# Gate and up projections by seven block products in place of eight, with sums of weight blocks made in DRAM, and a down projection in two groups

## The chip, the cores and the metric

The kernel runs on one core of one Trainium2 chip. The metric is the device time of one execution in microseconds (us), here the median of several runs. Engines: TensorE (PE in the profile; its weight loads PEld), VectorE (DVE), ScalarE (ACT), GpSimd (POOL) and SyncE (SP, which here only issues DMA).

## The reference

One layer of a decoder over 512 prompt tokens and 8 sample tokens (T = 520), model width 1024. Two attention mixers run on the same normalised input; the last part is what the change touches:

```python
m = gate_a * (oa @ w_pa) + gate_b * (ob @ w_pb)
x = x + m @ w_o
gu = _rmsnorm(x, norm2_g) @ w_gu              # w_gu [1024, 2 * 2816]
return x + (silu(gu[..., :D_FF]) * gu[..., D_FF:]) @ w_down
```

A final RMSNorm follows. Outputs are also the state rows of the caches (46 MB that only move along, DRAM to DRAM). All data is float32.

## The kernel before, in words

Everything is kept with features on the partitions and the 520 tokens along the free axis, in two halves of 256 and 264 columns (`SPAN`). A float32 product is made of three products of a rounded type: each operand is split into a high part and a low part, and `project_steps` issues high × high (L245), high × low (L246) and low × high (L248), for each of the chunks of 128 of the contraction and each half of the tokens.

The weights come as a list of `jobs`, one per block of 1024 × 128 (512 KB). For each job SP loads the block into one of three raw buffers (`load_plain`, L119), ScalarE makes the high part (`split_plain`, L137, `whi`) and VectorE the low part (L138, `wlo`). `weights(name)` queues the next job's split and up to four loads ahead. With each split `issue_copy` adds a rate to a counter, and whenever that passes 1 one of the 64 state copies is issued from ScalarE's queue (L112); `COPY_RATE` is 0.2 per job at first and 0.65 from job 44.

The stages from the middle on: the branch products with `w_pa` (PSUM tiles `pspa`, sums L1057 to L1060), the output projection with `w_o` (`pso`, residual L1089), norm 2 in two halves, then SwiGLU and down. Norm 2 takes the sum of squares per token on TensorE, its root on GpSimd (L1118, `rt`), spreads it by TensorE (`psr`), and VectorE makes the product with the gain (L1128, `h2f`), ScalarE and VectorE split it (L1129, L1130).

SwiGLU goes over 22 chunks of 128 features. Each has a gate and an up block: 8 chunks of contraction × 3 products × 2 halves = 48 matmuls each, 96 together (`psg`, `psu`). `gated` then takes silu on ScalarE (L1155), the product of gate and up on VectorE (L1156), and the split of the result (L1157, L1158), once for each half. Down is 8 output chunks m, each over all 22 chunks of features: 22 × 6 = 132 matmuls and two additions to the residual `x2` (L1266); the pieces of the final norm follow from `finish`, `emit` and `emit_last`.

A scheduler of the framework sets the order of the instructions on each engine from the program's order and its own estimates, before the kernel runs; each engine then works its list strictly in order, and waits where an instruction's inputs or buffers aren't ready.

Of the kernel before, what the change touches and what calls it, by code (L numbers as in the profile page):

```python
# [16 lines left out]
P = 128  # L17
# [6 lines left out]
SPAN = ((0, 256), (256, T))  # L24
HD = 64
# [11 lines left out]
COPY_FROM = 44  # L37
COPY_RATE = (0.2, 0.65)
# [14 lines left out]
POOLW = ("qb0", "qb1")  # L53


def trunk_kernel(tc, x_prompt, x_sample, cache_a, cache_b1, cache_b2, cache_b3, norm1_g, w_in, sinks,
# [8 lines left out]
    # ------------------------------------------------------------------ pools  # L65
# [14 lines left out]
    # ------------------------------------------------------------------ constants  # L80
# [10 lines left out]
    # ------------------------------------------------------------------ weights  # L91
    copies = []
    for b in range(NS):
# [5 lines left out]
        for r in range(0, 2047, 512):  # L99
            e = min(r + 512, 2047)  # L100
            copies.append((o_sb3[0, b, r:e], cache_b3[0, b, r + 1:e + 1]))
    copies.reverse()
    due = [0.0]

    def issue_copy(after, n):
        """State rows that only move along: DRAM to DRAM, paced by the weights."""
        due[0] += n
        with tc.issue_after(after.ins):
            while due[0] >= 1.0 and copies:
                due[0] -= 1.0  # L110
                o, i = copies.pop()
                nc.scalar.dma_start(o.rearrange("r a h d -> r (a h d)"), i.rearrange("r a h d -> r (a h d)"))  # L112
# [31 lines left out]
    def split_ff(raws, kc, name):  # L144
        return split_plain(raws, kc, name, pools["ff"], 2)

    def split_rope(cols):
        """Per 64-wide head a column offset; head dims d go to partition 2*(d%32)+d//32."""
# [15 lines left out]
    jobs = []  # (name, chunks of the contraction, loads, split)  # L164
# [48 lines left out]
    def split_to(n):  # L213
        while n_split[0] < min(n, len(jobs)):
# [4 lines left out]
            issue_copy(a, COPY_RATE[0 if i < COPY_FROM else 1])  # L219
# [3 lines left out]
    def weights(name, ahead=1):  # L223
        """Split weights of a job; the next job's split and the loads after it are queued first."""
# [56 lines left out]
    # ------------------------------------------------------------------ norm 1  # L281
# [48 lines left out]
    def norm_roots():  # L330
        """Per token the root of its mean square, as the diagonal of a matrix."""
# [15 lines left out]
    def half_x(h):  # L347
        """x of 256 tokens transposed, its product with the gain in two parts; the root per token comes after the projections."""
# [61 lines left out]
    # ------------------------------------------------------------------ pools of the two mixers  # L410
# [10 lines left out]
    def rope(ps2, dst, name, blocked=False):  # L421
        """ps2: PSUM [128, 2, 260]; dst [128, 520] gets the rotated values, prompt part in stride-4 blocks if asked."""
# [5 lines left out]
        nc.gpsimd.tensor_tensor(z, z, cos, op=ALU.mult)  # L428
# [745 lines left out]
    for m in range(2, NF):  # L1174
# [3 lines left out]
        for h in range(2):  # L1178
            gated(m, h, pgs[h], pus[h])
# [173 lines left out]
```

## Time and profile before

| | us |
|---|---|
| three runs | 918.91, 913.42, 915.9 |
| median | 915.9 |
| profiled execution, span from the first to the last instruction | 910.4 |
| TensorE busy in it | 883.6 |
| VectorE, ScalarE, GpSimd busy | 453.2, 340.4, 138.8 |
| DMA moved | 137.09 MB |

The profiled execution's span leaves out what lies before its first and after its last instruction, and is 5.5 us below the median of the runs. In the rows that the prediction shows, a group's row reads: line, engine, operation, output<-input, shapes, count | busy us in total, mean ns of one | idle us of the engine just before them and what ended it. A DMA row: what, queue, count, KB of each, median us from issue to landing. A window's row: from:to, length, busy us and count of each engine, the clock granted to TensorE, the share of the core's 16 DMA engines in use, GB/s. Matmuls overlap, so a matmul's own duration is longer than the time from one to the next.

### The profile page before, as it was taken

What the parts mean: (1) busy time and instruction counts of PE and PEld (TensorE: products, weight loads), DVE (VectorE), ACT (ScalarE), POOL (GpSimd) and SP (SyncE); (2) the same over time, 40 slices, a digit from 0 to 9 for tenths busy, and PEclk for the clock granted to TensorE, in tenths of its full rate; (3) what the DMA queues carried; (4) which work ended last, traced back from release to release, by engine and by line L of the source; (5) the groups of instructions that cost most, each with busy time, mean ns of one, the idle gap of its engine ahead of it and who ended that gap; (6) DMA issues with size and microseconds to landing.
All of it is one profiled execution on the core that took longest, in us unless ns stands there. A gap on an engine that the chain in (4) does not pass through costs nothing.

```text
span 910.4 us, 17130 instructions
## 1 busy us (share of the span) xinstructions
PE 883.6 (97%) x7104; PEld 833.4 (92%) x7104; DVE 453.2 (50%) x920; ACT 340.4 (37%) x750; POOL 138.8 (15%) x114
## 2 busy tenths in 40 slices
PE   6998989999999999999999999999999999999996
PEld 6898889878998788779999999999999999999995
DVE  4878648754597554724464653333333333233322
ACT  6324324444466655533233443222222222222222
POOL 2335553423232112100000200000000000000000
PEclk9999999999999999999999999999999999999998
DMA  9546745331332211488568339357356555657302
GB/s 298 174 129 189 216 147 181 100 99 47 94 117 94 72 32 60 124 195 233 157 208 272 93 114 278 113 184 229 114 177 194 155 167 174 194 162 235 90 19 95
DMA packets 149854, 137.09 MB, mean 151 GB/s; under 512 B 5344, under 2 KB 144768, under 8 KB 148368
## 3 DMA queue, kind: packets, MB, share of 16 engines
q1 hardware_dynamic: 145472, 83.65, 33.0%
q10 hardware_dynamic: 2592, 46.08, 14.7%
q0 software_dynamic: 1712, 6.26, 2.1%
q8 instruction: 56, 0.92, 0.4%
q14 instruction: 22, 0.18, 0.1%
HBM read 129.14 MB, written 51.86 MB: 199 GB/s over the span
## 4 chain that ended last, share of the span: by engine, by line
PE 83%; DMA 6%; DVE 5%; issue 3%; POOL 2%; ACT 1%; SPq 0%; POOLq 0%; DVEq 0%; ACTq 0%
PE psu L246 5%; PE psu L248 5%; PE psg L248 5%; PE psu L245 5%; PE psg L246 5%; PE psg L245 5%; PE psd L245 4%; PE psd L248 4%; PE psd L246 4%; PE poa L931 3%; DMA raw_wo<-in_w_o 2%; DMA qc<-q_dram 2%; PE psgb L248 2%; PE psgb L245 2%; PE psgb L246 2%
## 5 line engine op out<-in xcount | busy, mean ns | idle before, releaser
L245 PE MATMUL psd<-g_hi,whi_wd 128*128 128x256 f32 (+1 forms) x352 | 93.4, 285 | 0.5 <-DVE x L1266 0.5
L246 PE MATMUL psd<-g_lo,whi_wd 128*128 128x256 f32 (+1 forms) x352 | 93.1, 282 | 0.0
L246 PE MATMUL psu<-h_lo,whi_wu 128*128 128x256 f32 (+1 forms) x352 | 93.0, 283 | 0.0
L246 PE MATMUL psg<-h_lo,whi_wg 128*128 128x256 f32 (+1 forms) x352 | 92.6, 282 | 0.0
L245 PE MATMUL psu<-h_hi,whi_wu 128*128 128x256 f32 (+1 forms) x352 | 92.1, 282 | 0.0
L245 PE MATMUL psg<-h_hi,whi_wg 128*128 128x256 f32 (+1 forms) x352 | 91.6, 282 | 0.0
L248 PE MATMUL psd<-g_hi,wlo_wd 128*128 128x256 f32 (+1 forms) x352 | 74.5, 283 | 0.0
L248 PE MATMUL psu<-h_hi,wlo_wu 128*128 128x256 f32 (+1 forms) x352 | 73.5, 283 | 0.0
L248 PE MATMUL psg<-h_hi,wlo_wg 128*128 128x256 f32 (+1 forms) x352 | 73.4, 282 | 0.0
L245 PEld LDWEIGHTS psd<-g_hi,whi_wd 128*128 128x128 f32 x352 | 66.3, 188 | 0.8 <-DVE x L1266 0.7
L245 PEld LDWEIGHTS psu<-h_hi,whi_wu 128*128 128x128 f32 x352 | 66.3, 188 | 0.0
L246 PEld LDWEIGHTS psd<-g_lo,whi_wd 128*128 128x128 f32 x352 | 66.2, 188 | 0.0
L245 PEld LDWEIGHTS psg<-h_hi,whi_wg 128*128 128x128 f32 x352 | 66.1, 188 | 0.0
L246 PEld LDWEIGHTS psu<-h_lo,whi_wu 128*128 128x128 f32 x352 | 66.1, 188 | 0.0
L246 PEld LDWEIGHTS psg<-h_lo,whi_wg 128*128 128x128 f32 x352 | 66.1, 188 | 0.0
L138 DVE TENSOR_TENSOR wlo_wg<-raw_wg,whi_wg 128x1024 fp32r<-128x1024 f32 x22 | 27.0, 1225 | 74.4 <-ACT whi_wg L137 69.8
L248 PEld LDWEIGHTS psd<-g_hi,wlo_wd 128*128 128x128 f32 x352 | 55.9, 188 | 0.0
L138 DVE TENSOR_TENSOR wlo_wd<-raw_wd,whi_wd 128x1024 fp32r<-128x1024 f32 (+1 forms) x24 | 27.3, 1137 | 57.1 <-ACT whi_wd L137 56.2
L248 PEld LDWEIGHTS psu<-h_hi,wlo_wu 128*128 128x128 f32 x352 | 55.6, 188 | 0.0
L248 PEld LDWEIGHTS psg<-h_hi,wlo_wg 128*128 128x128 f32 x352 | 55.6, 188 | 0.0
L137 ACT ACTIVATE whi_wd<-raw_wd 128x1024 fp32r<-128x1024 f32 (+1 forms) x24 | 23.7, 989 | 84.6 <-PE psd L246 67.9
L1156 DVE TENSOR_TENSOR sg<-sg,psu 128x256 f32<-128x256 f32 (+1 forms) x44 | 16.9, 421 | 72.5 <-PE psu L248 72.5
(371 smaller groups left out, 2465.6 us busy)
## 6 DMA issues: line engine op xcount, KB each, us to landing
raw_wg<-in_w_gu SPq DMA_DIRECT2D x22, 512.0 KB, 3.9
raw_wu<-in_w_gu SPq DMA_DIRECT2D x22, 512.0 KB, 5.3
raw_wd<-in_w_down SPq DMA_DIRECT2D x16, 512.0 KB, 5.5
out<-in_cache_b_kv ACTq DMA_DIRECT2D x8, 1022.0 KB, 5.5
out<-in_cache_b_kv ACTq DMA_DIRECT2D x8, 512.0 KB, 4.0
raw_qa<-in_w_in SPq DMA_DIRECT2D x8, 512.0 KB, 3.8
raw_ga<-in_w_in SPq DMA_DIRECT2D x8, 512.0 KB, 4.8
raw_gb<-in_w_in SPq DMA_DIRECT2D x8, 512.0 KB, 3.9
```

Of the source, the lines that this page charges most:

```text
L137: a = nc.scalar.activation(hi[:, :kc], raw[:, :kc], AF.Copy)
L138: nc.vector.tensor_tensor(lo[:, :kc], raw[:, :kc], hi[:, :kc].bitcast(F32), op=ALU.subtract)
L245: nc.tensor.matmul(ps[i], hi[:, k], xh[:, k0 + k, sl], start=st, stop=False)
L246: nc.tensor.matmul(ps[i], hi[:, k], xl[:, k0 + k, sl], start=False, stop=False)
L248: last_mm[0] = nc.tensor.matmul(ps[i], lo[:, k], xh[:, k0 + k, sl], start=False, stop=en).ins
L931: nc.tensor.matmul(po[64 * kv:64 * kv + 64, :], va[:, j - 1 + r, 64 * kv:64 * kv + 64], pts_[kv, r], start=(r == rel[0]), stop=(r == 1), s ...
L1156: nc.vector.tensor_tensor(sg, sg, pu, op=ALU.mult)
```

## The change

Tokens: from the output projection on the halves are 260 and 260 columns (`SPAN2`). Norm 2 writes its result in quarters: two halves of the features times two halves of the tokens (`hq`, `hb_hi`, `hb_lo`).

Gate and up: chunks 0 and 1 (`NCL = 2`) are computed as before. For each of the other 20 ("units" 2 to 21) the gate block and the up block, each cut in two along the contraction, and the two token halves form a 2 × 2 block product, which is computed with seven block products (q1 to q7) in place of eight. A product is 4 chunks × 3 matmuls of 260 columns: 12; a unit 84. Three of the seven use a block of `w_gu` as it stands, four use a sum of blocks: s1 = a21 + a22, s2 = a11 + s1, s3 = a11 + a21, s4 = a12 + s2 (with signs put into the token side). These sums are made in DRAM: four tensors of 512 × 2560, each in four row blocks of 1.31 MB, by 16 plain copies on ScalarE's queue and 16 adding transfers on GpSimd's queue (`add_rows`). They are entries ahead of the 64 state copies in the same paced list, 96 in all. An adding transfer waits until its copy, and any sum that it reads, is there. The pace is 0.3 per job, 1.0 from job 18, 0.8 from job 56, then 0.15 per piece of a unit and 1.2 per piece of down.

The token side needs sums too: `sums_of_tokens` makes four sums of 1040 columns on VectorE, and splits four results on ScalarE and VectorE. The products' results are combined on VectorE (L1371 to L1382), with three activations on ScalarE (L1369, L1377, L1381) and one split of 520 columns (L1245, L1246).

A piece is a tile that holds the blocks of two products (two loads of 256 KB, L1313) or a block of down; four raw buffers and four pairs of `whi`/`wlo` hold them (L1325, L1326). Unit loads become 70 tiles of 512 KB where 40 blocks were.

Down: after unit 9 all 8 output chunks m are taken over the feature chunks 0 to 7 (48 matmuls each), and at the end all 8 over chunks 8 to 21 (84 each). So each m adds to `x2` twice.

The core of the diff:

```diff
+HH = T // 2
+SPAN2 = ((0, HH), (HH, T))
...
-COPY_RATE = (0.2, 0.65)
...
+NCL = 2
+SUM_RATE = (0.3, 1.0, 0.8)
+SUM_FROM, SUM_TO = 18, 56
+STEP_RATE = {"u": 0.15, "d": 1.2}
...
+    sums_d = {q: dram.tile([512, WS], F32, name=f"sum_{q}") for q in ("s1", "s2", "s3", "s4")}
...
+    sums = sum_step("s1", "a21", 0) + sum_step("s3", "a11", 0) + sum_step("s1", "a22", 1) + sum_step("s2", "a11", 0)
+    sums += sum_step("s3", "a21", 1) + sum_step("s4", "a12", 0) + sum_step("s2", "s1", 1) + sum_step("s4", "s2", 1)
+    copies = sums + copies
...
+    def add_rows(dst, src, r, add):
+        o, i = (quarter[n][P * r:P * r + P] for n in (dst, src))
+        if add:
+            with tc.issue_after(last_pool[0]):
+                last_pool[0] = nc.gpsimd.dma_start(o, i, accum_op=ALU.add, max_dma_last_dim=4 * WS // 2).ins
+        else:
+            nc.scalar.dma_start(o, i)
...
-            issue_copy(a, COPY_RATE[0 if i < COPY_FROM else 1])
+            issue_copy(a, SUM_RATE[(i >= SUM_FROM) + (i >= SUM_TO)])
...
+    AQ = {"q1": "a11", "q2": "a12", "q3": "s4", "q4": "a22", "q5": "s1", "q6": "s2", "q7": "s3"}
...
+        tt(hq[:, 0], hq[:, 0], hq[:, 3], op=ALU.subtract)
+        split(0)
+        yield
+        tt(hq[:, 3], hq[:, 3], hq[:, 2], op=ALU.subtract)
+        tt(hq[:, 2], hq[:, 2], hq[:, 0], op=ALU.add)
+        split(2)
+        yield
+        tt(hq[:, 1], hq[:, 1], hq[:, 2], op=ALU.subtract)
+        split(1)
+        split(3)
...
+            back = [("u", n - 1, "q3")] if n > a else []
+            steps_ += [("u", n, "q1")] + back + [("u", n, q) for q in ("q5", "q6", "q4", "q7", "q2")]
+        steps_.append(("u", b - 1, "q3"))
+        for m in range(NK):
+            steps_ += [("d", m, k0) for k0 in ((0,) if a == NCL else (FIRST, FIRST + 8))]
...
+            raw = pool.tile([P, NK, P], F32, tag="raw", name=f"rawp{i}", bufs=bufs)
+            k = 0
+            for _, src, kc in pieces[i]:
+                nc.sync.dma_start(raw[:, k:k + kc], src.rearrange("(k p) n -> p k n", p=P))
...
+        i = piece_of[s]
+        load_pieces(i + 4)
+        split_pieces(i + 3)
+        load_pieces(i + 5)
+        return w_of.pop(s)
...
+            if q == "q1":
+                nc.scalar.activation(self.s1, self.a, AF.Copy)
+            if q == "q6":
+                tt(self.v, self.b, self.s1, op=sub)
+            if q == "q7":
+                tt(self.c21, self.b, self.s1, op=sub)
+                tt(self.c22, self.c21, self.e, op=sub)
+                tt(self.c21, self.c21, self.f, op=add)
+            if q == "q2":
+                nc.scalar.activation(self.s1, self.a, AF.Silu)
+                tt(self.c21, self.c21, self.s1, op=ALU.mult)
+            if q == "q3":
+                tt(self.v, self.e, self.v, op=sub)
+                nc.scalar.activation(self.v, self.v, AF.Silu)
+                tt(self.c22, self.c22, self.v, op=ALU.mult)
+                split_g(self.n, self.z)
...
-            project(pds, weights(f"wd{m}_{k0}"), kc, g_hi, g_lo, k0=k0, first=k0 == 0, last=k0 + kc == NF)
+            project_d(pds, operand(s), 0, n, (0, 1), True, True)
```

How the order of the instructions changes is shown at three places. First VectorE in the steady part of gate and up. In before, for chunks 7 to 10 (`sg` the gated product, its two digits' last the half; `wlo_wg`, `wlo_wu` the low parts of the gate and up blocks):

```order
L138 TENSOR_TENSOR wlo_wg9_6876<-raw_wg9_0_6750,whi_wg9_6875 128x1024
L1156 TENSOR_TENSOR sg70_6805<-sg70_6805,psu70_6694 128x256
L1156 TENSOR_TENSOR sg71_6810<-sg71_6810,psu71_6695 128x264
L138 TENSOR_TENSOR wlo_wu9_6943<-raw_wu9_0_6818,whi_wu9_6942 128x1024
L1158 TENSOR_TENSOR g_lo_5779<-sg70_6805,g_hi_5778 128x256
L1158 TENSOR_TENSOR g_lo_5779<-sg71_6810,g_hi_5778 128x264
L138 TENSOR_TENSOR wlo_wg10_6998<-raw_wg10_0_6873,whi_wg10_6997 128x1024
```

In the changed kernel, for units 6 and 7 (`zs`, `z` the work tiles of a unit, `psa`, `psb`, `psf` PSUM banks, `wlo20` the low part of piece 20):

```order
L1371 TENSOR_TENSOR zs7_6742<-psb7_6802,zs7_6742 128x260
L1326 TENSOR_TENSOR wlo20_6784<-rawp20_6709,whi20_6783 128x1024
L1378 TENSOR_TENSOR z6_6620<-z6_6620,zs6_6619 128x260
L1326 TENSOR_TENSOR wlo22_6852<-rawp22_6787,whi22_6851 128x1024
L1373 TENSOR_TENSOR z7_6743<-psb7_6802,zs7_6742 128x260
L1326 TENSOR_TENSOR wlo23_6889<-rawp23_6821,whi23_6888 128x1024
L1380 TENSOR_TENSOR zs6_6619<-psa6_6618,zs6_6619 128x260
L1374 TENSOR_TENSOR z7_6743<-z7_6743,psa7_6741 128x260
L1326 TENSOR_TENSOR wlo21_6818<-rawp21_6748,whi21_6817 128x1024
L1375 TENSOR_TENSOR z7_6743<-z7_6743,psf7_6816 128x260
L1382 TENSOR_TENSOR z6_6620<-z6_6620,zs6_6619 128x260
L1246 TENSOR_TENSOR g81_6780<-z6_6620,g80_6779 128x520
```

Where a chunk had four short operations and two splits of weights, a unit has eight and three or four, the operations of two units are interleaved, and the pieces are not always split in the order of their numbers.

Second, GpSimd from the end of the attention of mixer A to norm 2. In before (`pa` attention probabilities, `rt0` the root of norm 2):

```order
L913 TENSOR_TENSOR pa121_3857<-pa121_3857,sta121_3858 128x1024
L913 TENSOR_TENSOR pa130_3943<-pa130_3943,sta130_3944 128x1024
L913 TENSOR_TENSOR pa131_4013<-pa131_4013,sta131_4014 128x1024
L1118 TENSOR_TENSOR rt0_5613<-rt0_5613,nhalf_91 128x3
L1130 TENSOR_TENSOR h2_lo_5401<-h2f01_5658,h2_hi_5400 128x256
```

In the changed kernel (`sum_s2`, `sum_s4` the tensors in DRAM):

```order
L947 TENSOR_TENSOR pa121_3878<-pa121_3878,sta121_3879 128x1024
L127 DMA sum_s2_97<-sum_s1_96 256x1280
L947 TENSOR_TENSOR pa130_3964<-pa130_3964,sta130_3965 128x1024
L947 TENSOR_TENSOR pa131_4035<-pa131_4035,sta131_4036 128x1024
L127 DMA sum_s2_97<-sum_s1_96 256x1280 x3
L127 DMA sum_s4_99<-sum_s2_97 256x1280 x4
L1163 TENSOR_TENSOR rt0_5654<-rt0_5654,nhalf_91 128x3
```

Eight of the sixteen adding transfers stand between the last attention products and the root of norm 2; the others stand among the attention's operations before.

Third, VectorE from norm 2's second half to the first units. In before (`dg1` the second half's diagonals, `h2f` its products with the gain):

```order
L1123 TENSOR_SCALAR dg11_5904<-ident_84,rt1_5839 128x128
L1123 TENSOR_SCALAR dg12_5907<-ident_84,rt1_5839 8x8
L1156 TENSOR_TENSOR sg00_5869<-sg00_5869,psu00_5810 128x256
L1158 TENSOR_TENSOR g_lo_5779<-sg00_5869,g_hi_5778 128x256
L1128 SCALAR_TENSOR_TENSOR h2f10_5910<-x2_4590,g2_95,psr1_5900 128x264
L1128 SCALAR_TENSOR_TENSOR h2f11_5914<-x2_4590,g2_95,psr1_5900 128x264
```

In the changed kernel, behind the eight products with the gain (`gcl` the gated product of a classical chunk, `ht_lo` low parts of the token sums):

```order
L1271 TENSOR_TENSOR hq_5438<-hq_5438 128x1040
L1265 TENSOR_TENSOR ht_lo_5988<-hq_5438,ht_hi_5987 128x1040
L1272 TENSOR_TENSOR hq_5438<-hq_5438 128x1040
L1265 TENSOR_TENSOR ht_lo_5988<-hq_5438,ht_hi_5987 128x1040
L1326 TENSOR_TENSOR wlo2_6135<-rawp2_5995,whi2_6134 128x1024
L1275 TENSOR_TENSOR hq_5438<-hq_5438 128x1040
L1215 TENSOR_TENSOR gcl0_5823<-gcl0_5823,psu01_6005 128x260
L1326 TENSOR_TENSOR wlo3_6168<-rawp3_5998,whi3_6167 128x1024
L1265 TENSOR_TENSOR ht_lo_5988<-hq_5438,ht_hi_5987 128x1040
L1215 TENSOR_TENSOR gcl1_5824<-gcl1_5824,psu11_6067 128x260
```

The token sums and their low parts stand between norm 2 and the first unit's own operations, mixed with the splits of the first pieces. Over the whole kernel TensorE has 3168 matmuls of 256 columns and 3072 of 264 in the projections of before, and 3312 of 260, 1392 of 256 and 1296 of 264 in the changed kernel.

More of the change, by code (lines that the diff above doesn't have):

```diff
@@ L36 @@
 FA = 0.6
-COPY_FROM = 44
-COPY_RATE = (0.2, 0.65)
 NWO = 5
@@ new lines, in classical @@
+    def classical(m, h):
+        pg, pu = banks(f"psg{m}{h}")[h], bank(f"psu{m}{h}")
+        project_q(pg, wgu[m][0], h)
+        if h == 0 and (m, 0) in NORM_AT:
+            next(norms[1], None)
+        project_q(pu, wgu[m][1], h)
+        if h == 0 and (m, 1) in NORM_AT:
+            next(norms[1], None)
+        g = gcl[m][:, HH * h:HH * h + HH]
+        nc.scalar.activation(g, pg, AF.Silu)
+        nc.vector.tensor_tensor(g, g, pu, op=ALU.mult)
+    for m in range(NCL):
+        classical(m, 0)
@@ new lines, in trunk_kernel, with yt_of, start_final @@
+    load_pieces(4)
+    tok_sums = sums_of_tokens()
+    next(tok_sums)
+    for m in range(NCL):
+        classical(m, 1)
+        split_pieces(m + 1)
+        next(tok_sums)
+        split_g(m, gcl[m])
+    fin_t = {}
+    def yt_of(j):
+        return fin_t["s"][:NS, 0] if j == 0 else fin_t["p"][:, j - 1]
+    tok = [(NP, NS)] + [(P * j, P) for j in range(4)]
+    ssq = fin.tile([P, 5, NK], F32, name="ssq")
+    ML = NK - 1
+    def start_final():
+        fin_t["p"] = hm.tile([P, 4, D], F32, tag="hm", name="ytp")
+        fin_t["s"] = hm.tile([P, 2, D], F32, tag="hm", name="yts")
+        nc.gpsimd.dma_start(fin_t["s"][:, 1], final_g.unsqueeze(0).to_broadcast([P, D]))
@@ new lines, in trunk_kernel, with project_d @@
+    ending = []
+    def project_d(ps, w, k0, m, hs, first, last):
+        hi, lo = w
+        kc = min(8, NF - k0)
+        for k in range(kc):
+            gh, gl = place(k0 + k)
+            st, en = first and k == 0, last and k == kc - 1
+            for h in hs:
+                sl = slice(*SPAN2[h])
+                nc.tensor.matmul(ps[h], hi[:, k], gh[:, sl], start=st, stop=False)
+                nc.tensor.matmul(ps[h], hi[:, k], gl[:, sl], start=False, stop=False)
+            for h in hs:
+                nc.tensor.matmul(ps[h], lo[:, k], gh[:, slice(*SPAN2[h])], start=False, stop=en)
+            if k in (3, 6) and ending:
+                ending.pop(0)()
@@ new lines, in trunk_kernel @@
+    units = {}
+    for s in steps_:
+        kind, n, q = s
+        if kind == "u":
+            if q == "q1":
+                units[n] = Unit(n)
+            units[n].run(q)
+        elif q == 0:
+            pds = pair(f"psd{n}")
+            project_d(pds, operand(s), 0, n, (0, 1), True, True)
+            for h in range(2):
+                down(n, h, pds[h])
+        elif q == FIRST:
+            if n == 0:
+                start_final()
+            pds = banks(f"pse{n}")
+            if n < NK - 1:
+                project_d(pds, operand(s), q, n, (0, 1), True, False)
+        elif n < NK - 1:
+            project_d(pds, operand(s), q, n, (0, 1), False, True)
+            for h in range(2):
+                down(n, h, pds[h])
+            ending += [lambda m=n: finish(m, (1, 2, 3, 4)), lambda m=n: finish(m, (0,))]
```

318 lines of the change are left out of this document (197 added, 121 removed).

## The prediction

> **What bounds the kernel now.** I read the head of the profile's page first: the span, the busy time of each engine, the DMA queues, and the engines' shares of the chain that ended last.
>
> ```profile
> span 910.4 us, 17130 instructions
> PE 883.6 (97%) x7104; PEld 833.4 (92%) x7104; DVE 453.2 (50%) x920; ACT 340.4 (37%) x750; POOL 138.8 (15%) x114
> ...
> q1 hardware_dynamic: 145472, 83.65, 33.0%
> q10 hardware_dynamic: 2592, 46.08, 14.7%
> ...
> PE 83%; DMA 6%; DVE 5%; issue 3%; POOL 2%; ACT 1%; SPq 0%; POOLq 0%; DVEq 0%; ACTq 0%
> ```
>
> TensorE is busy for 97% of the span and is 83% of the chain. Nothing else is near: VectorE is at half. q1 (SP's loads) moved 83.65 MB in 33.0% of 910.4 us, that is 278 GB/s while it runs; q10 (ACT's state copies) 46.08 MB in 14.7%, 344 GB/s. Then the stages that the change touches, by windows: the branch products (from 406), the output projection (466), norm 2 beside the first two gate/up chunks (514), the steady chunks (545 to 769), down.
>
> ```profile
> core 0: us, PE busy (x) PEld busy (x) DVE busy (x) ACT busy (x) POOL busy (x), PEclk, DMA share, GB/s
> ...
> 406.00:466.00 60.00, 60.00 (x489) 58.45 (x488) 28.46 (x38) 17.62 (x23) 0.00 (x0) 1.00 0.68 191
> 466.00:514.00 48.00, 46.62 (x389) 46.41 (x388) 27.86 (x55) 18.15 (x32) 3.13 (x4) 1.00 0.67 206
> 514.00:545.00 31.00, 31.00 (x260) 30.81 (x259) 17.88 (x39) 13.15 (x25) 2.33 (x2) 1.00 0.37 108
> 545.00:769.00 224.00, 224.00 (x1870) 224.00 (x1869) 76.44 (x117) 64.84 (x119) 0.00 (x0) 1.00 0.59 180
> ...
> 785.00:901.00 116.00, 115.38 (x963) 114.82 (x962) 37.67 (x81) 31.19 (x94) 0.72 (x1) 1.00 0.39 116
> ```
>
> From 545 to 769 TensorE never stops, at a granted clock of 1.00. So there each matmul removed is time removed, until another engine or the loads are late. The list of waits says how little TensorE waits in these stages today:
>
> ```profile
> PE pso L245 <- DVE x L1089: 1.4, 1, 1.4
> ...
> PE psd L245 <- DVE x L1266: 0.5, 1, 0.5
> ```
>
> **The change part by part. 1. Fewer matmuls.** The price of one comes from the period of a chunk, two neighbouring rows of VectorE's timeline:
>
> ```profile
> 562.00 0.76 DVE L1156 TENSOR_TENSOR sg<-sg,psu 128x256 f32<-128x256 f32 x2 [3.63 <-PE psu L248]
> 573.52 0.76 DVE L1156 TENSOR_TENSOR sg<-sg,psu 128x256 f32<-128x256 f32 x2 [3.63 <-PE psu L248]
> ```
>
> 573.52 − 562.00 = 11.52 us for 96 matmuls of 256 and 264 columns: 0.120 us each, and 260 columns is their mean. 20 chunks go from 96 to 7 × 12 = 84: 240 fewer, **−28.8 us**; a unit should take 84 × 0.120 = 10.08 us. Down keeps its 132 per m. [...]
>
> **2. More work on VectorE and ScalarE in each unit.** The groups of before:
>
> ```profile
> L138 DVE TENSOR_TENSOR wlo_wg<-raw_wg,whi_wg 128x1024 fp32r<-128x1024 f32 x22 | 27.0, 1225 | 74.4 <-ACT whi_wg L137 69.8 <-PE psg L246 4.6
> L137 ACT ACTIVATE whi_wg<-raw_wg 128x1024 fp32r<-128x1024 f32 x22 | 23.3, 1061 | 77.9 <-PE psg L246 73.4 <-DMA raw_wg<-in_w_gu 4.6
> L1156 DVE TENSOR_TENSOR sg<-sg,psu 128x256 f32<-128x256 f32 x22 | 9.3, 421 | 72.5 <-PE psu L248 72.5
> L1155 ACT ACTIVATE sg<-psg 128x264 f32<-128x264 f32 x22 | 8.5, 384 | 0.0
> L1058 DVE TENSOR_TENSOR ta<-ta,tb 128x520 f32<-128x520 f32 x8 | 5.6, 699 | 0.3
> L1059 ACT ACTIVATE m_hi<-ta 128x520 fp32r<-128x520 f32 x8 | 5.1, 641 | 5.0 <-DVE ta L1058 5.0
> ```
>
> VectorE per unit: seven operations on half the tokens at 0.421 (2.95), one on all 520 at 0.699, and 3.5 weight splits at 1.225 (4.29): 7.9 us of 10.08, 79%. ScalarE: 3 × 0.384 + 0.641 + 3.5 × 1.061 = 5.5 us, 55%. Both fit, so TensorE stays the bound of a steady unit. The chain inside a unit (product, subtraction, next product into the same bank) lies beside other banks' products, which the order interleaves. Taken: 0, and less slack for whatever comes late.
>
> **3. The start of the units.** VectorE ends norm 2's second half before any token sum can be made:
>
> ```profile
> 525.20 0.89 DVE L1128 SCALAR_TENSOR_TENSOR h2f<-x,g,psr 128x264 f32<-128x264 f32 x2 [0.44 <-PE psr L1124]
> 531.83 1.01 DVE L1130 TENSOR_TENSOR h_lo<-h2f,h_hi 128x264 fp32r<-128x264 f32 x2
> 541.23 0.42 DVE L1156 TENSOR_TENSOR sg<-sg,psu 128x264 f32<-128x264 f32 x1
> ```
>
> From 525.2 its order now holds, up to the first v (L1371 of unit 2): 8 products with the gain at 0.445 and 8 low parts at 0.42 (6.9 us); 4 token sums and 4 low parts of 1040 columns, 1.24 each (between 520 columns at 0.699 and 1024 at 1.225 a column costs 1.04 ns), 9.9; 5 weight splits, 6.1; 3 gate products, 1.3; two splits of g, 1.4. That sums to 25.6 us, so v comes at about 551. TensorE ends the second halves of the two classical chunks at about 541 (row 541.23 takes their last product), and its order puts 86 matmuls of units 2 and 3, 10.3 us, before the first that needs v: 551. A tie, with no slack: each wait on ScalarE's splits between (four of 1040 columns) adds. Bounds: 1 us (the tie holds but for one handover of 1.4 as in the waits above) to 11 (all of that 10.3 us cover lost). **+4 taken**, nearer the tie.
>
> **4. Weights in time.** Landing times of before, the median from issue to landing:
>
> ```profile
> raw_wg<-in_w_gu SPq DMA_DIRECT2D x22, 512.0 KB, 3.9
> raw_wu<-in_w_gu SPq DMA_DIRECT2D x22, 512.0 KB, 5.3
> raw_wd<-in_w_down SPq DMA_DIRECT2D x16, 512.0 KB, 5.5
> out<-in_cache_b_kv ACTq DMA_DIRECT2D x8, 1022.0 KB, 5.5
> ...
> raw_pa<-in_w_pa SPq DMA_DIRECT2D x16, 256.0 KB, 7.7
> ...
> qc<-q_dram POOLq DMA_DIRECT2D x6, 512.0 KB, 5.6
> ```
>
> A unit eats 3.5 pieces of 512 KB in 10.08 us, one each 2.88 us; four raw buffers make a turn of 11.5 us. Of that go 1.06 and 1.23 for the two splits and about 3 us (one piece's time; my choice) in which the split waits its turn on two in-order engines: some 6 us are left for a load. 3.9 to 5.5 fits, 7.7 doesn't. What the DMA engines must do: 1.84 MB per 10.08 us at 278 GB/s is 65%, and half a state copy (0.38 MB at 344 GB/s) 11%: 76%, against 0.59 now and 0.67 where raw_pa needed 7.7. So loads land nearer 6 than 4, some late. Bounds: 0, and 17.5 turns × 1.15 us (two thirds of the way from 6 to 7.7) = 20. **+5 taken.**
>
> **5. The sums of weight blocks.** 16 plain copies and 16 adding transfers of 1.31 MB. Their issue is hidden: POOL's queue has nothing between its last attention product and norm 2's root, and an issue costs ACT's queue half a microsecond.
>
> ```profile
> 382.52 1.91 POOL L913 TENSOR_TENSOR pa<-pa,sta 128x1024 f32<-128x1024 f32 x1 [4.70 <-ACT pta L925]
> 504.10 0.90 POOL L1118 TENSOR_TENSOR rt<-rt,nhalf 128x3 f32<-128x3 f32 x1 [119.67 <-DVE rt L1117]
> ...
> 556.06 0.52 ACTq L112 DMA_DIRECT2D out<-in_cache_b_kv  x1
> ```
>
> If that cover went, 16 × 0.52 = 8.3 us of ScalarE's queue would show. No row of before is an adding transfer. By the nearest rows 1.31 MB takes from 3.8 us (q10's 344 GB/s) to 14 (qc's 512 KB in 5.6, from POOL). I take the middle, 7 to 9: it reads two blocks and writes one. The last eight (s2, then s4) run from about 385, and 8 × 9 = 72 us end them by 460. But this lies in the stretch of 0.68 share, with more state copies there too (1.0 and 0.8 a job where 0.65 was), so pa and wo weights come later than now, where TensorE lost 1.4. Bounds: 0 (state copies give way) to 12 (eight adds at 1.5 us of extra weight delay each, about a quarter of qc's 5.6). **+3 taken.** The Trainium skill ("Collectives: The Full Stack", section "The bandwidth ceiling: the fold count and why AG ≠ RS ≠ AR") says that an add is slowed by its two source reads, to about half the rate of a copy; on that estimate the middle of my bounds, not the lower end, is right, and no run here shows it yet.
>
> **6. Down in two groups.** Same matmuls; eight more pairs of additions to x (0.42 each on a VectorE that is a third busy) lie beside them. The two switches between units and down drain the pipe of pieces for a moment. Group two loads 14 blocks per m in 84 × 0.120 = 10.1 us and copies 1.2 state rows per piece: 0.92 MB at 278 plus 1.7 MB at 344 GB/s are 8.3 us of 10.1, 82%. Bounds 0 to 3, **+1 taken.** The tail after the last matmul (900.93 to the end) is unchanged:
>
> ```profile
> 900.93 0.43 DVE L1266 TENSOR_TENSOR x<-x,psd 128x264 f32<-128x264 f32 x1 [1.63 <-PE psd L248]
> ...
> 906.09 0.30 SPq L1262 DMA_DIRECT2D out<-yts  x1
> ```
>
> **Sum:** −28.8 + 4 + 5 + 3 + 1 = −15.8. The profiled execution's 910.4 becomes 894.6. The span lies 5.5 below the median of the runs (915.9), and I carry the difference over: 915.9 − 15.8 = 900.1, so **900 us**.
>
> **The rivals.**
>
> *All hidden.* Loads land in 5 us as raw_wu does and the start ties: −28.8 + 0 to 4 gives 887 to 891. For it: 224 us without one wait today. Against it: four buffers at 76% DMA share, and part 3's tie.
>
> *Loads too late.* If pieces land at raw_pa's 7.7 us, each turn of four buffers is 1 to 1.7 us longer than TensorE's, over 17.5 turns 18 to 30 us in place of my 5: 913 to 925. For it: the share of 0.67 at which raw_pa needed that. Against it: raw_pa is two issues on 64 partitions each, and raw_wd landed in 5.5 in a stretch of mixed load. Also ScalarE and VectorE take pieces out of turn where the order says so, so one late piece holds the rest.
>
> *Slower: the adds are slow.* The place is POOL's queue: the four s4 adds stand in it waiting for the s2 adds, and norm 2's root (504) stands behind them. And unit 2's third product wants s4 loaded by about 533, where norm 2 ends. From 385 that leaves 148 us, 18.5 us for each of eight adds in a row: this is the point from which it decides. At 25 us each the eight end 52 us late: about 950. For it: adds are nowhere in the trace and share the engines with weights at 0.68. Against it: 18.5 us is above even the 14 of qc's pace, and adds may overlap. The Trainium skill ("DMA: Bandwidth & Descriptors", section "Issuing engines are not separate DMA queues") says that transfers of SP, ACT and GpSimd run on the same 16 engines and interleave, which speaks against this change: adds from POOL take from SP's weights. The windows agree so far that the share is one pool (0.68 while SP and ACT both issue).
>
> *The change doesn't do what it says* would need the matmuls to stay; the order of the new kernel has 240 fewer, so I give that 1%.
>
> **How the numbers follow.** The forecast's case 0.58, 892 to 908 by the bounds of parts 3 to 6 taken partly together; all hidden 0.12; loads too late 0.15; slow adds 0.14. 0.5% is 4.6 us, about what a measurement of this kernel can tell from no change: faster is below 911.3, slower above 920.5. Faster: 0.58 + 0.12 = 0.70. Loads too late falls to both sides of 920.5: 0.09 same, 0.06 slower, and 1% for no effect is same: 0.10. Slower: 0.06 + 0.14 = 0.20. The range goes from the lower end of all hidden, 887, into the late loads at 920, which leaves out slow adds and the upper end of late loads, just under 0.2.
>
> **What would show it.** In the new trace: units of 10.1 to 10.4 us between two L1382 rows; TensorE's waits under L1350 summing to under 12 us, with 2 to 6 of it at the first units on VectorE's L1371; landing of pieces at 5 to 6.5 us and a DMA share of 0.7 to 0.8 in the units; the adds landing in under 18 us each, the last before 500; no wait of the root on POOL. It is wrong if units take 11 us or more (late loads, or VectorE over its 79%), if norm 2 starts later than at 504 plus 5, or if TensorE waits in the branch or output projections for over 12 us.

## The result, and the profile after

The changed kernel takes 947.85 us (median of 4 runs, 940.25 to 953.12); before stands at 915.53 in the same runs. The ratio is 1.035, interval 1.030 to 1.040: slower by 3.5%, where 900 was forecast. The profiled execution has a span of 945.9 us, 35.5 above before's 910.4. Its own time was 947.66, 1.8 us more than its span, and in the later runs the two lie as far apart. So of the 5.5 us between before's span and its median only about 1.8 would lie outside the span (an estimate): its profiled execution was a quick one, and the differences between the two traces below are some 3 us larger than the 32.3 between the medians.

The page of the changed kernel, the lines that were read of before:

```profile
span 945.9 us, 17102 instructions
PE 870.8 (92%) x6868; PEld 816.5 (86%) x6868; DVE 539.8 (57%) x1054; ACT 381.8 (40%) x782; POOL 158.6 (17%) x130
...
PEclk9999999999999999957899999999999999999998
...
q1 hardware_dynamic: 177792, 99.39, 37.9%
q10 hardware_dynamic: 4896, 67.06, 20.0%
q0 software_dynamic: 6064, 27.23, 13.8%
...
PE 70%; DMA 11%; DVE 6%; issue 3%; ACT 2%; POOL 2%; another core or an unknown queue 1%; ACTq 0%; POOLq 0%; DVEq 0%; SPq 0%
```

TensorE does less (870.8 us for 883.6) and the time is longer: it now waits. DMA went from 6% to 11% of the chain, and the granted clock, at nine tenths or more in every slice but the last before, falls to 0.5 in one place in the middle. Its list of waits:

```profile
PE ta L957 <- ACT pta L959: 21.3, 1, 21.3
PE pspa L279 <- ACT whi_pa L170: 9.6, 1, 9.6
...
PE psa L1350 <- ACT zs L1369: 8.3, 5, 2.7
...
PE psb L1350 <- ACT whi L1325: 3.1, 3, 1.0
```

By the first matmul of each stage the time goes like this (a stage's row in the view of a tile, here that of the gate in the changed kernel, ends with the first and the last start):

```profile
L1195 PE MATMUL psg<-hb_hi,whi_wg x32: 277/282/288, 559.7 to 583.5; 128*128 128x260 f32 x32
```

| first matmul of | before | after | later by |
|---|---|---|---|
| branch products | 407.0 | 444.9 | 37.9 |
| output projection | 465.7 | 511.8 | 46.1 |
| gate and up | 514.3 | 559.7 | 45.4 |
| (end) last sum of down | 900.9 | 936.2 | 35.3 |

So the loss, 45 us in the traces, is complete before a single one of the new products is computed. From gate and up to the end the changed kernel gains 10 us, where 28.8 less the losses of parts 3, 4 and 6 (10) were forecast to leave 19.

What holds the 21.3 us is in the chain of waits around 386, on ScalarE's timeline at its end, in the issues on GpSimd's and SP's queues, and in two windows of 5 us. The chain:

```profile
386.80 34.65 DMA raw_ga<-in_w_in
421.53 0.54 ACT whi_ga L170
...
422.50 0.59 ACT pta L959
423.13 1.11 PE ta L957 x4
```

GpSimd's queue, from the end of the attention:

```profile
385.70 3.61 POOL L127 DMA_DIRECT2D sum_s<-sum_s  x4
400.40 0.87 POOL L127 DMA_DIRECT2D sum_s<-sum_s  x1 [11.09 <-issue]
407.14 0.88 POOL L127 DMA_DIRECT2D sum_s<-sum_s  x1 [5.87 <-issue]
413.90 0.87 POOL L127 DMA_DIRECT2D sum_s<-sum_s  x1 [5.88 <-issue]
```

SP's queue in the same time, where before an issue of raw_ga took 0.37 us in the median and one of raw_pa 0.65:

```profile
389.39 15.47 SPq L160 DMA_DIRECT2D raw_pa<-in_w_pa  x2
404.96 12.55 SPq L152 DMA_DIRECT2D raw_ga<-in_w_in  x1
```

And the windows:

```profile
405.00:410.00 5.00, 0.00 (x0) 0.00 (x0) 0.00 (x0) 0.00 (x0) 0.88 (x1) 0.64 1.05 214
410.00:415.00 5.00, 0.00 (x0) 0.00 (x0) 0.00 (x0) 0.00 (x0) 0.87 (x1) 0.50 1.06 216
```

From 386 the adding transfers hold all 16 engines (share 1.05). One add ends every 6.75 us (the last three issues wait for one each: 400.40, 407.14, 413.90), which is 1.31 MB in 6.75, 194 GB/s. The windows show 215: some 20 GB/s are left for the weights. The 512 KB of raw_ga, for which ScalarE and behind it the attention's last pieces and TensorE wait, take 34.65 us, where before a block of raw_ga took 4.8 in the median. And with TensorE idle, its clock is granted at 0.64, then 0.50; from 420 to 480, with more waits, the windows of 5 and 10 us show it between 0.50 and 1.00, and from 480 on at 1.00.

### The profile page after: what moved, and what is told of

Read it like the earlier page. It is cut to its first block, busy times and chain, and to the rows that moved or that the text cites. A ratio compares the mean times of both kernels' runs of the same rounds, so it can differ in the third digit from the quotient of the medians.

```text
span 945.9 us, 17102 instructions
## 1 busy us (share of the span) xinstructions
PE 870.8 (92%) x6868; PEld 816.5 (86%) x6868; DVE 539.8 (57%) x1054; ACT 381.8 (40%) x782; POOL 158.6 (17%) x130
## 3 DMA queue, kind: packets, MB, share of 16 engines
q1 hardware_dynamic: 177792, 99.39, 37.9%
## 4 chain that ended last, share of the span: by engine, by line
PE 70%; DMA 11%; DVE 6%; issue 3%; ACT 2%; POOL 2%; another core or an unknown queue 1%; ACTq 0%; POOLq 0%; DVEq 0%; SPq 0%
DMA raw_ga<-in_w_in 4%; PE psa L1350 4%; PE psa L1351 3%; PE psa L1352 3%; PE pse L1493 3%; PE pse L1494 3%; PE pse L1496 3%; PE poa L965 3%; DMA rawp<-sum_s 2%; DMA qc<-q_dram 2%; PE psgb L282 2%; PE pspa L282 2%; PE psb L1350 2%; PE pspa L279 2%; PE psgb L280 2%
## 5 line engine op out<-in xcount | busy, mean ns | idle before, releaser
L1325 ACT ACTIVATE whi<-rawp 128x1024 fp32r<-128x1024 f32 (+1 forms) x94 | 97.7, 1041 | 146.0 <-PE psa L1351 53.6
L1326 DVE TENSOR_TENSOR wlo<-rawp,whi 128x1024 fp32r<-128x1024 f32 (+1 forms) x94 | 112.7, 1200 | 51.6 <-ACT whi L1325 51.1
L1350 PE MATMUL psa<-hb_hi,whi 128*128 128x260 f32 x240 | 67.9, 283 | 0.0
L1351 PE MATMUL psa<-hb_lo,whi 128*128 128x260 f32 x240 | 67.8, 282 | 0.0
L1352 PE MATMUL psa<-hb_hi,wlo 128*128 128x260 f32 x240 | 67.6, 282 | 0.0
L1493 PE MATMUL pse<-g,whi 128*128 128x260 f32 x224 | 60.7, 290 | 1.2 <-DVE x L1481 0.7
L1494 PE MATMUL pse<-g,whi 128*128 128x260 f32 x224 | 59.4, 283 | 0.0
L1350 PE MATMUL psb<-ht_hi,whi 128*128 128x260 f32 x160 | 45.8, 286 | 3.7 <-ACT whi L1325 3.1
L1496 PE MATMUL pse<-g,wlo 128*128 128x260 f32 x224 | 47.7, 283 | 0.0
L1351 PE MATMUL psb<-ht_lo,whi 128*128 128x260 f32 x160 | 45.3, 283 | 0.0
L1493 PEld LDWEIGHTS pse<-g,whi 128*128 128x128 f32 x224 | 42.1, 188 | 1.7 <-DVE x L1481 0.9
L1494 PEld LDWEIGHTS pse<-g,whi 128*128 128x128 f32 x224 | 42.2, 188 | 0.0
L957 PE MATMUL ta<-ident,pa 128*128 128x128 f32 x112 | 17.8, 281 | 21.4 <-ACT pta L959 21.3
## 6 DMA issues: line engine op xcount, KB each, us to landing
sum_s<-in_w_gu POOLq DMA_DIRECT2D x8, 1280.0 KB, 10.1
```

What stands on the lines that cost most here:

```text
L1325: a = nc.scalar.activation(hi, raw[:, :kc], AF.Copy)
L1326: nc.vector.tensor_tensor(lo, raw[:, :kc], hi.bitcast(F32), op=ALU.subtract)
L1350: nc.tensor.matmul(ps, hi[:, i], xh[:, j, i], start=start and i == 0, stop=False, skip_group_check=True)
L1351: nc.tensor.matmul(ps, hi[:, i], xl[:, j, i], start=False, stop=False, skip_group_check=True)
L1352: nc.tensor.matmul(ps, lo[:, i], xh[:, j, i], start=False, stop=i == 3, skip_group_check=True)
L1493: nc.tensor.matmul(ps[h], hi[:, k], gh[:, sl], start=st, stop=False)
```

## The experiments

Theory A: the adds keep the weights away. Rivals: B, the faster pace of the state copies does; C, the units themselves cost more; and for the units, D and E below.

**The last eight adds left out.**

```diff
-        if add:
+        if add and dst in ("s2", "s4"):
+            return
+        if add:
```

> The changed kernel without its last eight adding transfers (those that make s2 and s4 from s1 and s2); the sums s2 and s4 then hold only their plain copies, so this part of the computation is left out. Theory A (the adds of 385 to 450 us keep TensorE's weights away): the branch products start at 407 to 412 in place of 444.9, no wait of 21 us on the attention's last pieces, and the time falls by 40 to 48 us to 900 to 908. Theory B (the faster pace of the state copies is what crowds out the weights): the branch products still start 25 us or more late, time above 930. Theory C (the units themselves cost more than the blocks they replace): time falls by less than 15.

902.82 us, ratio to before 0.983 (0.979 to 0.987). The branch products:

```profile
L281 PE MATMUL pspa<-oa_hi,whi_pa x128: 276/281/290, 405.6 to 463.8; 128*128 128x256 f32 x64, 128*128 128x264 f32 x64
```

They start at 405.6, 1.4 us earlier than before, at the same pace of state copies. The first eight adds (162 to 284 us) cost nothing that this start shows. A holds, B and C fall for the loss of 45 us.

**The sums alone, on the kernel before.** The edit puts the change's list of sums, its `add_rows` and its paces into the kernel before; the gate and up projections stay as they are.

> The kernel before with the 16 copies and 16 adding transfers of the change at the same places and the same pace of the list, and nothing else of the change; the sums are made and not used. Theory A: it is slower than before by the whole loss up to the branch products and output projection, 38 to 48 us: 953 to 963, with a wait of about 20 us in front of the same attention piece. Theory C (units at fault): slower by under 15 us.

953.79 us, ratio 1.039 (1.035 to 1.043), that is 36.6 us over the before of these runs, and the wait is at the same place:

```profile
PE ta L952 <- ACT pta L954: 21.8, 1, 21.8
PE pspa L274 <- ACT whi_pa L166: 11.2, 1, 11.2
```

The loss needs nothing of the new products.

**Smaller pieces of the adds.**

```diff
-                last_pool[0] = nc.gpsimd.dma_start(o, i, accum_op=ALU.add, max_dma_last_dim=4 * WS // 2).ins
+                last_pool[0] = nc.gpsimd.dma_start(o, i, accum_op=ALU.add, max_dma_last_dim=4 * WS // 10).ins
```

> The changed kernel with the adding transfers cut into pieces of 1024 bytes in place of 5120, at the same places in GpSimd's queue. Theory A1 (each DMA engine takes one piece of an add and one 512-byte row of a weight block in turn, so that weights get a tenth of the bytes): the raw_ga block that took 34.7 us lands in under 15, and the time falls by 20 us or more if the adds' own rate holds; if smaller pieces make the adds themselves two to five times slower, they last to 500 or beyond and less is gained, but the weights still get a third of the bytes. Theory A2 (the volume of the adds is what counts, whatever its pieces): raw_ga still lands after 30 us or more and the time stays within 5 us of 948.

940.14 us, ratio 1.024 (1.020 to 1.029). The block of raw_ga that the attention waits for, issued at 389.97, is there at 406.0, after 16 us in place of 35 (the chain, then ScalarE's timeline), while the adds take longer (landing, and queue 0 of the page):

```profile
389.97 15.96 DMA raw_ga<-in_w_in
```

```profile
406.01 1.06 ACT L170 ACTIVATE whi_ga<-raw_ga 128x1024 fp32r<-128x1024 f32 x1 [7.32 <-DMA raw_ga<-in_w_in]
```

```profile
sum_s<-sum_s POOLq DMA_DIRECT2D x8, 1280.0 KB, 44.9
```

```profile
q0 software_dynamic: 22448, 27.23, 16.5%
```

The DMA records of the two traces can be counted by queue. While that block was under way, the engines worked 1133 pieces of adds and 1204 rows of weights in the change (386.8 to 421.5), and 1515 and 1419 here (389.97 to 406.0). So about one row of 512 bytes goes for one piece of an add, of 5120 bytes there and of 1024 here: the engines serve the two queues piece by piece, not byte by byte. In bytes that is 20 GB/s of weights beside 194 from 403 to 421 in the change, one to ten, and 68 beside 139 from 405 to 410 here, the third of the bytes that A1 named. So A1's mechanism holds and A2 falls, though 16 us is just over A1's 15. But the adds didn't keep their rate (139 GB/s, and less where state copies run too: the issues of the last three are 12 and 15 us apart), and the same volume has to go through: the branch products, which had taken 67 us, now start at 422.0 and take 85, and the output projection starts at 507.0, 4.8 us earlier than in the change. So the 20 us of gain, which A1 had tied to that rate, did not come, only 8; the size of the pieces decides who waits, the volume how long. The Trainium skill ("DMA: Bandwidth & Descriptors", section "SWDGE vs HWDGE vs iDMA") says that GpSimd's transfers and those of SP and ScalarE feed different internal queues of each engine, between which the engine goes round robin; the 20 to 194 agrees with that.

**Other places for the adds.** Three kernels move the adds, and with the pace also the plain copies of the sums and the state copies. First a faster pace from the start:

```diff
-SUM_RATE = (0.3, 1.0, 0.8)
+SUM_RATE = (0.6, 1.3, 0.7)
```

> The changed kernel with a faster pace of the paced list at first (0.6, 1.3, 0.7 for 0.3, 1.0, 0.8): the sums start earlier, and the last eight adds stand one by one between the products of the attention of mixer A, no longer eight in a row behind them. Theory A: the first eight adds of the changed kernel, spread from 165 to 288 us, stopped nobody; spread like them, the other eight won't either: branch products start at 407 to 418, time 900 to 915. Theory B (state copies): those come at least as early here, so time stays above 930. Where the adds still meet each other, waits of a few us appear on whi_gb or whi_ga before 380.

927.28 us, ratio 1.011 (1.007 to 1.015): 20 us better than the change, 12 to 27 us worse than expected. The branch products start at 440.3, where 407 to 418 was expected, and then take 57.6 us; from gate and up to the end it is 7 us shorter than the change. Beside the last eight adds, now mostly one by one from 268 to 344, TensorE has no wait over 0.2 us. But four of the first ones now stand in a row at 101 us, and there the same happens to a block of mixer B's weights (raw_vb takes 31.35 us in the chain, from 105.34), with TensorE's wait behind it:

```profile
101.50 4.73 POOL L127 DMA_DIRECT2D sum_s<-in_w_gu  x4
```

```profile
PE psvb L279 <- ACT whi_vb L170: 9.6, 1, 9.6
PE pspb L279 <- ACT whi_pb L170: 8.7, 1, 8.7
```

The second wait has no add near it: a block of 128 KB (raw_pb) takes 17.24 us in the chain of waits, from 399.88, behind five state copies that the faster pace issues between 389.6 and 398.2. So theory B isn't nothing: copies in a row do the same for a shorter time.

Second, slow up to job 17, then fast:

```diff
-SUM_RATE = (0.3, 1.0, 0.8)
-SUM_FROM, SUM_TO = 18, 56
-STEP_RATE = {"u": 0.15, "d": 1.2}
+SUM_RATE = (0.3, 1.6, 0.65)
+SUM_FROM, SUM_TO = 18, 35
+STEP_RATE = {"u": 0.17, "d": 1.5}
```

> The changed kernel with the paced list slow up to job 17 (0.3, as in the change), fast from job 18 to 34 (1.6) and 0.65 behind that; 0.17 and 1.5 per piece. All sixteen adds then stand between about 165 and 340 us, mostly singly between GpSimd's attention work, and neither in a row at 100 us (as in spread_adds) nor behind the attention (as in the change). Theory A (adds hurt where they come in a row while a weight block is wanted): no wait over 3 us on a weight split before the branch products, which start at 405 to 415; time 900 to 912. If single adds hurt too (any add delays the load beside it by its own 7 us, and slack there is less than that), waits on whi_qa, whi_gb or whi_pb sum to 15 us or more, and time is 920 or more.

939.99 us, ratio 1.028 (1.018 to 1.037). A miss: four adds stand within 20 us from 157 on, beside the loads of the caches; one of these (vc) takes 37.04 us in the chain, from 163.55, and TensorE waits there as long as in the change at 400:

```profile
PE sb L799 <- DVE stb L807: 23.1, 1, 23.1
```

```profile
163.55 37.04 DMA vc<-in_cache_b_kv
```

Third, the last eight by the attention's own beat, with a pace of 0.3, 1.3 and 0.8 for the rest of the list:

```diff
...
+    adds_left = [c[1:] for c in sums if c[4] and c[1] in ("s2", "s4")]
+    n_mult = [0]
+    copies = [c for c in sums if c[1:] not in adds_left] + copies
...
+        n_mult[0] += 1
+        if n_mult[0] % 2 == 0 and adds_left:
+            add_rows(*adds_left.pop(0))
```

> The changed kernel with the first eight adding transfers where they are or slightly earlier, and each of the last eight behind every second product of GpSimd in the attention of mixer A (10 us apart from 310 to 385), by no pace; the plain copies and state copies on the paced list (0.3, 1.3 from job 18, 0.8 from job 34, then 0.15 and 1.3). Theory A in its narrower form (two or more adds in flight take a weight block's share of the engines; one at a time, 7 us of engine time in every 10, leaves the loads of the attention stages enough): branch products at 405 to 412, no wait over 4 us before them, time 900 to 908. If even single adds 10 us apart delay the blocks (raw_gb, raw_pb) by more than their slack: waits of 10 us or more on whi_gb and whi_pb, time 915 or more, and the narrower form falls.

939.2 us, ratio 1.023 (1.018 to 1.028). The narrower form of A falls. Three adds 9 and 10 us apart, with two plain copies of the sums issued beside them at 285.35 and 296.34, are enough (GpSimd's queue, then the chain):

```profile
289.84 0.93 POOL L129 DMA_DIRECT2D sum_s<-sum_s  x1
299.07 0.89 POOL L129 DMA_DIRECT2D sum_s<-sum_s  x1
308.66 0.94 POOL L129 DMA_DIRECT2D sum_s<-sum_s  x1
```

```profile
289.02 34.22 DMA raw_gb<-in_w_in
```

An add lands after 13.6 us in the median here, so at 9 to 10 us apart there is always one in flight, and a block beside them again takes 34 us. How much of it the two plain copies took was not tested. What cost nothing were the first eight adds of the change, from 165 to 288 us; they are 7 to 53 us apart, so distance alone doesn't decide. That it is what is loaded beside them, and how soon it is wanted, is my reading and not shown. No place was found for all sixteen.

**The units' own loss.** To measure it I added up, over neighbouring matmuls from the first gate product to the end, by how much more than 0.12 us the next one starts later (where it is over 0.08): 1.9 us before, 21.4 in the change. The picture of one such loss, on ScalarE's timeline and then on TensorE's:

```profile
737.16 0.42 ACT L1381 ACTIVATE zs<-zs 128x260 f32<-128x260 f32 x1 [0.27 <-DVE zs L1380]
742.39 1.06 ACT L1325 ACTIVATE whi<-rawp 128x1024 fp32r<-128x1024 f32 x1 [4.81 <-DMA rawp<-sum_s]
743.35 0.62 ACT L1245 ACTIVATE g<-z 128x520 fp32r<-128x520 f32 x1
743.88 0.37 ACT L1369 ACTIVATE zs<-psa 128x260 f32<-128x260 f32 x1
```

```profile
744.29 0.58 PE L1350 MATMUL psa<-ht_hi,whi 128*128 128x260 f32 x1 [2.66 <-ACT zs L1369]
```

A split waits 4.81 us for its piece; the short copy of a product (L1369), which has its input, stands behind it on ScalarE, and TensorE waits for that copy to get its bank back.

Without state copies beside the units:

```diff
-STEP_RATE = {"u": 0.15, "d": 1.2}
+STEP_RATE = {"u": 0.0, "d": 1.65}
```

> The changed kernel with no state copies while the units run (0 per piece), and 1.65 per piece of down in place of 1.2. Theory D (state copies crowd the units' loads): TensorE's lost time in the units falls from about 18 us to under 8, and the time to 935 to 940. Theory E (four raw buffers, which the order fills in bursts, leave a load too little time whatever else runs): lost time stays over 13 us, time 945 to 952; down's loads may get later by a few us under either.

946.97 us, ratio 1.034 (1.028 to 1.040), lost 21.8 us: D falls. With six raw buffers:

```diff
-            pool, bufs = (ffp, 1) if i % 4 == 0 else (wp, RAW)
+            pool, bufs = (ffp, 3) if i % 2 == 0 else (wp, RAW)
...
-        load_pieces(i + 4)
+        load_pieces(i + 6)
...
-        load_pieces(i + 5)
+        load_pieces(i + 7)
```

> The changed kernel with six raw buffers for the pieces in place of four, loads queued two pieces further ahead; nothing else. Theory E (the units lose time because a load that the order starts late, in a burst, holds ScalarE's queue and with it the copy of the product that frees a bank): the wait of TensorE on L1369 falls from 8.3 to under 3 us, the units' lost time from 21 to 10 to 14 us, time 936 to 942. If the units' losses come from the handover between product, VectorE and the same bank, they stay: 945 to 951.

934.89 us, ratio 1.020 (1.016 to 1.025), lost 10.1 us, and the wait on the copy is nearly gone:

```profile
PE psa L1350 <- ACT zs L1369: 1.3, 2, 0.8
```

E holds for half of the loss; what the other 10 us are stays open. Together with the adds by the attention's beat:

> Both together: adds one at a time and six raw buffers. If both theories hold, the gains add: 890 to 900, faster than before by 2 to 3%.

932.53 us, ratio 1.018 (1.014 to 1.022), a miss, since 890 to 900 was expected: the units' gain is there (11.3 us lost), the adds' isn't, for the reason above.

**Sums without adding transfers.** The blocks a11, a12, a21, a22 of a unit are loaded, and GpSimd adds them in SBUF:

```diff
+        add(sm["q5"], b[:, :4], b[:, 4:], op=ALU.add)
+        add(sm["q6"], a[:, :4], sm["q5"], op=ALU.add)
+        add(sm["q7"], a[:, :4], b[:, :4], op=ALU.add)
+        add(sm["q3"], a[:, 4:], sm["q6"], op=ALU.add)
```

> The seven block products as in the change, but the four sums of weight blocks of a unit are made in SBUF by GpSimd from the unit's four loaded blocks (four additions of 128 x 512 per unit): no copies and no adding transfers in DRAM, 40 loads of 512 KB for the units in place of 70, the pace of the state copies before the units as in the kernel before, then 0.3 and 1.0 per piece. Each split of a product's block is one operation of 512 columns, seven each per unit on ScalarE and VectorE. Theory A with E (the whole loss is DMA: adds first, late loads second): branch products at 407, units at 10.1 to 10.6 us each, 888 to 898. If the units' loss is VectorE's and ScalarE's queues and not the loads (VectorE now at about 8.5 of 10.1 us): units at 11 us or more, 903 to 915.

930.83 us, ratio 1.016 (1.011 to 1.022): a miss by over 30 us. The branch products start at 407.6, as in the kernel before, so the adds' loss is gone; but 45.6 us are lost in the units. VectorE's timeline, and its groups with GpSimd's:

```profile
740.51 0.68 DVE L1332 TENSOR_TENSOR wlo<-sq,whi 128x512 fp32r<-128x512 f32 x1
...
744.99 1.77 DVE L1332 TENSOR_TENSOR wlo<-rawp,whi 128x512 fp32r<-128x512 f32 x1
746.68 0.41 DVE L1381 TENSOR_TENSOR z<-z,psa 128x260 f32<-128x260 f32 x1
```

```profile
L1332 DVE TENSOR_TENSOR wlo<-rawp,whi 128x512 fp32r<-128x512 f32 x60 | 61.4, 1032 | 12.6 <-ACT whi L1331 12.4
...
L1307 POOL TENSOR_TENSOR sq<-rawp,rawp 128x512 f32<-128x512 f32 x20 | 32.9, 1645 | 9.5 <-DVE wlo L1332 9.5
...
L1381 DVE TENSOR_TENSOR z<-z,psa 128x260 f32<-128x260 f32 x20 | 8.4, 420 | 0.4
```

The same split takes 0.68 us with GpSimd idle and up to 1.77 while it adds; operations with one input in PSUM keep their 0.42. VectorE, estimated at 8.5 of 10.1 us per unit, is busy for 116.71 of 133 us from 697 to 830 (88%), which leaves the in-order queues little slack.

**A version that beats both.** s1 and s3 stay in DRAM, with the eight adds where they cost nothing; s2 and s4 are made per unit in SBUF, with five raw buffers, once by VectorE and once by GpSimd:

```diff
+        add = nc.vector.tensor_tensor
+        add(sm["q6"], a[:, :4], b[:, :4], op=ALU.add)
+        add(sm["q3"], a[:, 4:], sm["q6"], op=ALU.add)
```

> The seven block products with only s1 and s3 made in DRAM (the eight adding transfers of 165 to 290 us, at the places where the change has them); s2 = a11 + s1 and s4 = a12 + s2 are made per unit in SBUF by VectorE, two additions of 128 x 512 at 0.69 us. Loads of a unit are 1.25 MB in place of 1.75, five raw buffers; each product's split is one operation of 512 columns. Theory A (only adds in a crowd and beside wanted weights cost): branch products at 405 to 408 as in no_late_adds. VectorE per unit: 7 x 0.42 + 0.70 + 7 x 0.69 + 2 x 0.69 = 9.9 us of 10.1, at its limit: units of 10.4 to 11 us, so 892 to 905, faster than before by 1 to 2.5%. If eight adds cost as such: branch products at 420 or later, no gain.

> The same with the two additions per unit on GpSimd. In sums_on_gpsimd four of them per unit took 1.4 to 1.6 us each, and VectorE's operations with both inputs in SBUF took up to 2.6 times as long beside them (1.77 for 0.69 us). With two per unit, 3 us of 10: VectorE at 8.5 + 3 x 0.7 = 10.5 us per unit in place of 9.9: units of 10.6 to 11.3, 897 to 910, slower than half_on_vector by 0 to 8. If the slowing were tied to something else than GpSimd at work, VectorE's split would stay at 0.69 and this kernel would be the faster of the two by 4 or more.

908.72 us, ratio 0.990 (0.986 to 0.993), and 909.98, 0.991 (0.989 to 0.994): both about 1% faster than before, and not to be told from each other. The first misses its 892 to 905 by 4 us, the second is in its range. In the groups, VectorE's splits take 0.688 us in the first; in the second, those of loaded blocks take 0.811, while the additions have left VectorE:

```profile
L1356 DVE TENSOR_TENSOR wlo<-rawp,whi 128x512 fp32r<-128x512 f32 x100 | 67.3, 688 | 20.9 <-ACT whi L1355 20.3
```

```profile
L1356 DVE TENSOR_TENSOR wlo<-rawp,whi 128x512 fp32r<-128x512 f32 x100 | 79.3, 811 | 19.7 <-ACT whi L1355 19.3
```

Both lose 21 us in the units, and their branch products start at 417.5 and 418.1, 12 us later than with no late adds, although the adds stand where they did. These two also issue the state copies sooner (no s2 and s4 stand in front of them in the list); that this is the reason was not tested.

## Why the prediction was wrong

**Part 1, the matmuls: right.** 240 fewer at 0.120 us; the units' matmuls still follow each other at 0.12, and with six raw buffers gate, up and down (560.0 to about 925) are 21 us shorter than before (514.3 to 900.9).

**Part 2, VectorE and ScalarE: right in that both fit.** The windows of the units in the changed kernel:

```profile
585.00:670.00 85.00, 79.49 (x650) 78.19 (x649) 59.98 (x92) 42.51 (x61) 0.00 (x0) 1.00 0.64 185
...
719.00:845.00 126.00, 118.53 (x967) 117.35 (x966) 80.83 (x128) 58.40 (x84) 0.00 (x0) 0.99 0.68 194
```

From 719 to 845 VectorE is busy for 80.83 of 126 us, 64%, and 71% in the first window, where 79% was put. What the balance left out is order: ScalarE's queue with 5.5 us of work in 10 still held a short copy behind a split that waited for DMA.

**Part 3, the start: +4 forecast, under 1 measured.** TensorE waits for nothing over 0.2 us from the first unit up to 610; the tie held.

**Part 4, late loads: the place right, the reason and the size wrong.** +5 was taken, the upper bound was 20, and the change lost about 19 with the switches of part 6. The share of the engines, from which I argued, wasn't the point: it is 0.64 to 0.68 in the units, under my 0.76, the loads of 256 KB land after 4.1 to 4.3 us in the median, and taking the state copies away changes nothing. My reading is that the order fills the four buffers in bursts, and that a burst that starts late makes one split late. Six buffers give back 11 of the 21 us, which bears it out for that half.

**Part 5, the sums: this is the step that failed.** "+3 taken", between 0 and 12, and the runs show 45 (no_late_adds) and 37 (sums_alone). The price of one add was right: 7 to 9 us were taken, and the trace has 6.75 (194 GB/s, 0.56 of the 344 of plain copies); and the eight were done by 447 (the last issue at 413.9 and the longest landing of 32.7), before the 460 that I gave. What was wrong is the bound, "eight adds at 1.5 us of extra weight delay each": by these two runs the eight cost 4.6 to 5.6 us each. I took it that a weight beside an add is delayed a little. While an add of 5120-byte pieces is in flight, a weight block gets one byte for ten of the add, so it waits for nearly the whole add. And I had put the eight adds' 72 us into a stretch in which the next weight is always wanted, with three raw buffers. One of the prediction's own signs of being wrong came with it: norm 2's root, due by 509, starts at 549.1.

**The rival "slow adds"** named 950 and a chance of 0.14, and the time came out there, but by luck and not for its reason: the adds were not slow, no add was late for s4, and norm 2's root did not wait on GpSimd. The rival "loads too late" had the right victim, with the wrong stage and price. What I wrote beside them, that adds from POOL take from SP's weights because the share is one pool, was the sentence to follow: if transfers that need all engines for 54 us (8 at 6.75) are put into a pool at 0.68, something must give way, and what TensorE waits for gave way.

The clock added to it: TensorE's idle stretch of 20 us was followed, up to 480, by windows in which the granted clock was down again (0.50 from 440 to 450, 0.89 and 0.77 from 460 to 480), and the branch products took 66.9 us for 58.7 from their first matmul to the output projection's. A wait of 3.1 us for whi_ga is in that; the other 5 us go with the lower clock, which no run tested by itself. The sum had no term for either.

## What to carry to other kernels

Price a bulk transfer not by its own time only but by what a needed load gets beside it. Here the load got one row for each piece of the bulk transfer: the 1024 rows of a block on 16 engines wait for 64 pieces each, which at 0.40 us a piece (the records of the adds) is 26 us of the 34.65, an estimate. See whether the load's buffers cover that. Work moved to an engine or queue that is idle on average is free only if it shares nothing with the one that sets the pace: here GpSimd's DMA shared the engines with the weights, and GpSimd's additions slowed VectorE's splits. And in-order queues turn a late input into a late everything: a balance of 55% says nothing about a short copy behind a split that waits.

## What the runs showed of the hardware

- An adding transfer in DRAM of 1.31 MB took 6.75 us of all 16 engines, 194 GB/s beside 20 GB/s of weights, where the plain state copies of before come to 344 GB/s over the time of their packets.
- In flight together, weights and adding transfers shared by pieces, about one for one (1204 rows to 1133 pieces, and 1419 to 1515): weights in rows of 512 bytes got 20 GB/s beside adds in pieces of 5120 (194 GB/s), and 68 beside pieces of 1024 (139 GB/s).
- VectorE's operation on two inputs in SBUF went from 0.68 to up to 1.77 us while GpSimd added in SBUF, and GpSimd's took 1.4 to 1.6; with one input in PSUM VectorE kept 0.42. The Trainium skill ("SBUF — State Buffer", section "Who interferes with whom") says that a VectorE instruction with two SBUF inputs contends with a GpSimd instruction that reads SBUF, and these rows agree.
- In the change TensorE is idle from about 402 to 423; the clock granted to it is 0.64 in the window 405 to 410, 0.50 in 410 to 425, 1.00 in 430 to 435, lower again with the next waits (0.50 in 440 to 450), and at 1.00 from 480 on.
